# Expert matmuls of the first layer in tiles of 32 columns, and the first modulation summed in PSUM

## The chip, the cores and the metric

The kernel runs on one core of a Trainium2 chip. The core has five engines that run side by side: TensorE for matmuls (its weight loads are shown apart), VectorE, ScalarE, GpSimd, and SyncE, whose queue issues most of the loads. Sixteen DMA engines move data between HBM and SBUF. Matmuls write to PSUM, which this kernel uses in banks of 128 partitions x 512 float32. The metric is the device time of one execution in microseconds.

## The reference

The reference is one mixing block followed by a two-layer block. All of it is float32, with D = 1024, 512 tokens (the latent ones) and 256 context tokens.

```python
# first block: modulation from the vector c, then norm, affine, projection
mod = silu(c) @ w_ada + b_ada                    # 1024 x 3072
shift, scale, gate = split(mod, 3)
h = rms_norm(x, norm_pre) * (1 + scale) + shift
proj = h @ w_in                                  # then a recurrence and an attention, w_out
...
# in each of two layers, behind its attention: 16 experts, each takes its top tokens
xs = h[idx]                                      # 64 latent tokens, 32 context tokens
a, u = xs @ w_gate[e], xs @ w_up[e]              # 1024 x 1024 each
y = (silu(a) * u) @ w_down[e]                    # 1024 x 1024
out = zeros.at[idx].add(y * gates)
```

In the first layer both latent and context tokens go through the experts (context with its own choice and the same weights); in the second layer only the latent ones do.

## The kernel before

The whole program is one launch. Code is written as generators that are woven together, and a planner puts every engine's instructions into a fixed order, so an engine's order follows the program's where nothing is blocked.

**Start of the first block** (`first`, lines 629 to 704). x is loaded in four tiles, then the first group of w_in (`group_`: load into a ring of two tiles `w`, copy on ScalarE into `hi`, subtraction on GpSimd into `lo`, because each projection is three matmuls on split operands, lines 323 to 325). Then the first modulation runs: `ada` (line 336) takes w_ada in tiles of 128 x 1024 (`wa`, 512 KB; two per k, sixteen for shift and scale) through a ring of four, and for each of eight k makes one matmul per half row (line 364) into column tiles of 32 of a PSUM bank. Here the bank comes from `held`, a pool of one; each k's result is added to `rows` on VectorE (line 366), which gives the bank back. At the end `done1` transposes the rows (line 378) into columns, and A and shift follow. Between the modulation's fourth step and its end stand the small tables: softplus, block weights `wbd`, position and rope tables, mask, then the norm of x and its transposes into `xT`. With A known, xT is scaled (line 698), copied to `h_hi` and subtracted to `h_lo` (lines 699 and 700; odd k on VectorE, even k on GpSimd), and the projection starts.

**Experts** (`experts`, line 1427). Per expert, X is gathered by an indirect DMA (line 1439), transposed (line 1445), and goes as the stationary operand XT (1024 rows in eight k; 64 latent and 32 context columns). Weights come in loads of 1 MB, two k each, through 19 slots (`slot`, line 1406): four pairs for gate and up, then four for down. A slot is loaded again when its matmuls are done. For each k the latent part makes four matmuls into two column tiles of 64 (line 1468) and the context part four into column tiles of 32 (line 1459), in turn; for the last two k the context part comes after both. Then silu on ScalarE, product on VectorE, transposes (lines 1481 and 1493), and the down matmuls: latent in tiles of 64 (line 1503), context in tiles of 32 (line 1518). Results are scaled and added to HBM by indirect DMAs on GpSimd's queue. Four PSUM banks rotate for gate, up, context and the context transposes.

## Time and profile before

| | |
|---|---|
| three runs | 2518.55, 2521.3, 2523.43 us (median 2521.3) |
| profiled execution | 2520.2 us |
| its span, first to last instruction | 2518.4 us |
| TensorE busy | 2134.2 us (85%) |
| TensorE weight loads | 1209.4 us (48%) |
| VectorE, ScalarE, GpSimd busy | 43%, 28%, 23% |
| moved by DMA | 563.86 MB, mean 224 GB/s |

Busy time is an average over stages. The first block and the attentions lie before 950 us and between 1520 and 1950 us, the first layer's experts between 957 and 1525 us, the second layer's between 2009 and 2510 us. A float32 matmul stands in the trace as two records, each with a weight load of its own. Names of engines in rows: PE is TensorE, PEld its weight loads, DVE VectorE, ACT ScalarE, POOL GpSimd, SPq the queue of loads.

### The profile page before, as it was taken

How to read it: one execution, taken by the hardware profiler on the slowest of the kernel's cores; microseconds unless marked ns; L12 is line 12 of the kernel's file. 1: busy time of each engine (PE TensorE's matmuls, PEld its weight loads, DVE VectorE, ACT ScalarE, POOL GpSimd, SP SyncE). 2: the span in 40 equal slices, each digit the busy share in tenths (PEclk: the TensorE clock that was granted, in tenths of full speed). 3: DMA queues.
4: the chain of work that ended last, by engine and by line, in shares of the span. 5: the costliest groups of instructions: out<-in, count | busy, mean ns of one | idle time of the engine just before them, and what ended most of it. 6: DMA issues, size and time to landing. Idle time of an engine off the chain costs nothing. (4 is left out here: it accounts for less than half of the span.)

```text
span 2518.4 us, 32647 instructions
## 1 busy us (share of the span) xinstructions
PE 2134.2 (85%) x12298; PEld 1209.4 (48%) x12298; DVE 1074.1 (43%) x2785; ACT 711.5 (28%) x1642; POOL 586.6 (23%) x804
## 2 busy tenths in 40 slices
PE   5999887999997868999999996599988597767677
PEld 1778666677785752222222224467677332212222
DVE  5476777646869461111111116788784500000000
ACT  3355543445546110000000004455664100000000
POOL 3343232331434311101111003433243200000000
PEclk9999897999998978999999998799999699998889
DMA  8441231422431558999999953033125699999997
GB/s 284 151 135 43 80 122 30 143 79 77 138 103 55 200 209 316 379 386 381 376 376 383 387 209 96 22 103 100 56 77 176 254 385 391 395 394 390 393 404 279
DMA packets 160761, 563.86 MB, mean 224 GB/s; under 512 B 16454, under 2 KB 16710, under 8 KB 160476
## 3 DMA queue, kind: packets, MB, share of 16 engines
q1 hardware_dynamic: 146172, 522.90, 55.8%
q0 software_dynamic: 14432, 38.88, 5.7%
q8 instruction: 97, 1.59, 0.3%
q14 instruction: 60, 0.49, 0.1%
HBM read 538.59 MB, written 23.14 MB: 223 GB/s over the span
## 5 line engine op out<-in xcount | busy, mean ns | idle before, releaser
L1468 PE MATMUL bank<-we,XT 128*64 128x512 f32 x2048 | 507.3, 629 | 94.7 <-DMA we<-in_w_exp_gate_dram 66.0
L1468 PEld LDWEIGHTS bank<-we,XT 128*64 128x64 f32 x2048 | 141.2, 142 | 442.1 <-issue 322.8
L1478 DVE TENSOR_TENSOR sg<-sg,bank 128x512 f32<-128x512 f32 x32 | 22.0, 687 | 646.5 <-PE bank L1468 646.5
L1503 PE MATMUL pbank<-we,hT 128*64 128x512 f32 x1024 | 229.1, 596 | 10.7 <-ACT hT L1483 9.0
L1477 ACT ACTIVATE sg<-bank 128x512 f32<-128x512 f32 x32 | 19.1, 597 | 661.0 <-PE bank L1468 661.0
L1439 POOL DMA_INDIRECT X<-H,gx x32 | 29.9, 934 | 617.6 <-PE bank L1445 553.7
L526 PE MATMUL bank<-cons,p 128*128 128x128 f32 x800 | 127.5, 282 | 27.2 <-ACT pT L252 10.2
L512 DVE TENSOR_REDUCE mx<-bank 128x1 f32<-128x768 f32 (+1 forms) x160 | 134.9, 846 | 35.8 <-PE bank L504 34.5
L515 ACT ACTIVATE p<-bank,mx 128x768 f32<-128x768 f32 (+1 forms) x160 | 130.7, 818 | 58.7 <-DVE mx L512 22.0
L1503 PEld LDWEIGHTS pbank<-we,hT 128*64 128x64 f32 x1024 | 71.5, 137 | 145.6 <-issue 126.2
L1459 PE MATMUL bank<-we,XT 128*32 128x512 f32 x1024 | 133.9, 607 | 0.0
L526 PEld LDWEIGHTS bank<-cons,p 128*128 128x128 f32 x800 | 92.4, 143 | 61.0 <-ACT pT L252 17.6
L268 POOL TENSOR_TENSOR lo<-w,hi 128x1024 fp32r<-128x1024 f32 (+1 forms) x44 | 95.2, 2170 | 98.1 <-ACT hi L267 66.2
L323 PE MATMUL pbank<-hi,h 128*128 128x384 f32 x288 | 101.7, 354 | 7.0 <-ACT vt L1094 3.6
L252 ACT ACTIVATE pT<-bank 128x256 f32<-128x256 f32 (+3 forms) x187 | 84.5, 476 | 70.2 <-PE bank L526 63.7
L325 PE MATMUL pbank<-hi,h 128*128 128x384 f32 x288 | 100.6, 349 | 0.0
L324 PE MATMUL pbank<-lo,h 128*128 128x384 f32 x288 | 100.3, 348 | 0.0
L1507 DVE SCALAR_TENSOR_TENSOR yl<-pbank,gt,m 128x512 f32<-128x512 f32 x32 | 23.9, 748 | 177.9 <-PE pbank L1503 151.5
L504 PE MATMUL bank<-ks,qs 128*128 128x256 f32 (+1 forms) x320 | 83.4, 375 | 12.5 <-ACT p L515 9.1
L268 POOL TENSOR_TENSOR wo_lo<-wo_raw,wo_hi 128x512 fp32r<-128x512 f32 (+1 forms) x40 | 60.7, 1527 | 99.6 <-ACT wo_hi L267 97.5
L504 PEld LDWEIGHTS bank<-ks,qs 128*128 128x128 f32 x320 | 57.1, 205 | 35.3 <-ACT p L515 14.5
L1483 ACT ACTIVATE hT<-pbank 128x512 f32<-128x512 f32 x32 | 19.1, 597 | 183.5 <-PE pbank L1481 183.5
(444 smaller groups left out, 4204.6 us busy)
## 6 DMA issues: line engine op xcount, KB each, us to landing
we<-in_w_exp_down_dram SPq DMA_DIRECT2D x127, 1024.0 KB
we<-in_w_exp_up_dram SPq DMA_DIRECT2D x124, 1024.0 KB
we<-in_w_exp_gate_dram SPq DMA_DIRECT2D x123, 1024.0 KB
wa<-in_w_ada_dram SPq DMA_DIRECT2D x120, 512.0 KB
w<-in_w_in_dram SPq DMA_DIRECT2D x24, 512.0 KB
w<-in_w_in_even_dram SPq DMA_DIRECT2D x20, 384.0 KB
H<-h SPq DMA_DIRECT2D x10, 512.0 KB
we<-in_w_exp_gate_dram POOLq DMA_DIRECT2D x5, 1024.0 KB, 10.9
```

Source lines behind the costliest of these rows:

```text
L252: self.nc.scalar.activation(out, ps, AF.Copy)
L268: (engine or self.nc.gpsimd).tensor_sub(lo, w, hi)
L323: t.matmul(ps, lhsT=lhs[0], rhs=rhs[0], start=start, stop=False)
L324: t.matmul(ps, lhsT=lhs[0], rhs=rhs[1], start=False, stop=False)
L325: t.matmul(ps, lhsT=lhs[1], rhs=rhs[0], start=False, stop=stop)
L504: self.nc.tensor.matmul(ps[:, a - k0:b - k0], lhsT=qs[:, q0:q0 + 128], rhs=ks[:, a:b], start=i == 0, stop=i == len(passes) - 1)
L512: nc.vector.tensor_reduce(m, ps, axis=AX, op=OP.max, negate=True)
L515: nc.scalar.activation(p, ps, AF.Exp, bias=m, accum_out=den)
L526: self.nc.tensor.transpose(ps[:, a - b:a - b + 128], p[:, a:a + 128], self.ident)
L1459: nc.tensor.matmul(pc[q:q + 32], lhsT=XT[:, k, 64:96], rhs=w[:, k % 2, 512 * h:512 * h + 512], start=k == 0, stop=k == 7)
L1468: nc.tensor.matmul(ps[64 * h:64 * h + 64], lhsT=XT[:, k, :64], rhs=w[:, k - k0, 512 * h:512 * h + 512], start=k == 0, stop=k == 7)
L1503: nc.tensor.matmul(py[64 * h:64 * h + 64], lhsT=hT[:, j, 64 * kh:64 * kh + 64], rhs=w[:, 512 * h:512 * h + 512], start=j == 0 and kh == 0, ...
```

## The change

In the first layer's experts, gate and up go into three banks. Each bank holds, for one group of 32 tokens (two groups latent, one context), up and gate in four column tiles of 32; in the second bank gate and up change places. All four column tiles are written in turn, and so are those of the down matmuls, for latent as for context. Silu and product run once for each bank. The second layer's experts keep their tiles of 64. In both layers the up weights of a pair are loaded before the gate weights, and the functions are split up.

In the first block the modulation's weights are loaded right behind x, through a ring of nine tiles, ahead of the first group of w_in, the tables and the block weights. Where a `held` bank is given, the sum over k stays in PSUM and is added to `rows` once. x is transposed into the tile Y, which is otherwise first written later.

```diff
@@ -333,12 +333,12 @@
                 yield


-    def ada(self, w, b, stat, nmod, nvec, pool, ring, banks, done, bank=None, bufs=None):
+    def ada(self, w, b, stat, nmod, nvec, pool, ring, banks, done, held=None, bufs=None):
+


         nc = self.nc
         wv = w.rearrange("(k p) n -> p k n", p=128)
-        bank = bank or self.pbank
         wt = [None, None]

         def load(bk, k):
@@ -359,11 +359,16 @@
             load(bk, 0)
             yield
             for k in range(8):
-                ps = bank()
+                if not held:
+                    ps = self.pbank()
+                elif k == 0:
+                    ps = held()
                 for t in range(2 * len(mods)):
                     nc.tensor.matmul(ps[32 * t:32 * t + 32, :], lhsT=stat[:, k, :],
-                                     rhs=wt[t // 2][:, (t % 2) * 512:(t % 2 + 1) * 512], start=True, stop=True)
-                nc.vector.tensor_add(rows[:n], ps[:n], rows[:n])
+                                     rhs=wt[t // 2][:, (t % 2) * 512:(t % 2 + 1) * 512],
+                                     start=not held or k == 0, stop=not held or k == 7)
+                if not held or k == 7:
+                    nc.vector.tensor_add(rows[:n], ps[:n], rows[:n])
                 if k < 7:
                     load(bk, k + 1)
                 yield
@@ -660,15 +665,32 @@
         mask = mk.tile([128, 512], F32, name="mask")
         k2 = self.pool("f_k2")
         xp = self.pool("f_x")
-        sring = self.pool("f_sring", 4)
+        sring = self.pool("f_sring", 9)
         xt = xp.tile([128, 4, D], F32, name="x")
         for t in range(4):
             nc.sync.dma_start(out=xt[:, t], in_=I["x"][t * 128:(t + 1) * 128, :])
         stat = self.stationary(self.col("c"), 1, "stat1", ap)
         ada1 = lambda banks, ring: self.ada(I["w_ada"], I["b_ada"], stat, 3, 1, ap, ring, banks, done1, held)
+        mods = ada1((0,), sring)
+        drain(take(mods, 5))
+        xT = Y[:, :, :S]
+        for t in range(4):
+            r = self.tile_rstd(xt[:, t], xp.tile([128, D], BF16, name="junk", bufs=1))
+            v.tensor_scalar(xt[:, t], xt[:, t], r, None, op0=OP.mult)
+        drain(take(mods, 2))
+        for k in range(8):
+            ps = self.bank()
+            for t in range(4):
+                nc.tensor.transpose(ps[:, t * 128:(t + 1) * 128], xt[:, t, k * 128:(k + 1) * 128], self.ident)
+            self.evac(xT[:, k], ps)
+        drain(mods)
         w = drain(self.group_(I["w_in_0"]))
-        mods = ada1((0,), sring)
-        drain(take(mods, 4))
+        for k in range(8):
+            v.tensor_scalar(xT[:, k], xT[:, k], A[:, k:k + 1], mod[:, 0, 0, k:k + 1], op0=OP.mult, op1=OP.add)
+            nc.scalar.activation(hi[:, k], xT[:, k], AF.Copy)
+            (v if k % 2 else nc.gpsimd).tensor_sub(lo[:, k], xT[:, k], hi[:, k])
+        sring.release()
+        xp.release()
         sp = self.softplus_neg(self.col("lam"), k2)
         spc = k2.tile([128, 2, 4], F32, name="spc")
         v.tensor_scalar(spc[:, 0], sp, 2.0, None, op0=OP.mult)
@@ -684,23 +706,6 @@
                 nc.sync.dma_start(out=wbd[64 * b:64 * b + 64, j, :, 64 * b:64 * b + 64], in_=wg[b])
         cs, sn = self.first_rope_tables(k2)
         nc.sync.dma_start(out=mask, in_=I["mask"])
-        xT = xp.tile([128, 8, S], F32, name="xT")
-        for t in range(4):
-            r = self.tile_rstd(xt[:, t], xp.tile([128, D], BF16, name="junk", bufs=1))
-            v.tensor_scalar(xt[:, t], xt[:, t], r, None, op0=OP.mult)
-        for k in range(8):
-            ps = self.bank()
-            for t in range(4):
-                nc.tensor.transpose(ps[:, t * 128:(t + 1) * 128], xt[:, t, k * 128:(k + 1) * 128], self.ident)
-            self.evac(xT[:, k], ps)
-        drain(mods)
-        for k in range(8):
-            v.tensor_scalar(xT[:, k], xT[:, k], A[:, k:k + 1], mod[:, 0, 0, k:k + 1], op0=OP.mult, op1=OP.add)
-            nc.scalar.activation(hi[:, k], xT[:, k], AF.Copy)
-            (v if k % 2 else nc.gpsimd).tensor_sub(lo[:, k], xT[:, k], hi[:, k])
-        sring.release()
-        xp.release()
-
         scr = self.pool("f_scr")
         sc = self.pool("f_sc", side="right")
         stk = self.pool("f_stk", 2, side="right")
@@ -1449,97 +1453,129 @@
...
-            pg, pu = self.bank(), self.bank()
-            pc = self.bank() if ctx else None
-
-            def gate_up_ctx(k, wg, wu):
-                for j, w in enumerate((wu, wg)):
-                    for h in range(2):
-                        q = 64 * j + 32 * h
-                        nc.tensor.matmul(pc[q:q + 32], lhsT=XT[:, k, 64:96],
-                                         rhs=w[:, k % 2, 512 * h:512 * h + 512], start=k == 0, stop=k == 7)
-
-            for k0 in range(0, 8, 2):
-                wg = load(I["w_exp_gate_2"][i, e], k0)
-                wu = load(I["w_exp_up_2"][i, e], k0)
-                for k in range(k0, k0 + 2):
-                    for ps, w in ((pg, wg), (pu, wu)):
-                        for h in range(2):
-                            nc.tensor.matmul(ps[64 * h:64 * h + 64], lhsT=XT[:, k, :64],
-                                             rhs=w[:, k - k0, 512 * h:512 * h + 512], start=k == 0, stop=k == 7)
-                    if ctx and k < 6:
-                        gate_up_ctx(k, wg, wu)
-            if ctx:
-                for k in (6, 7):
-                    gate_up_ctx(k, wg, wu)
...
+            last = e + 1 == EXPERTS
+            XT = (self.expert_ctx if ctx else self.expert_lat)(i, e, R, wk, XT, None if last else prep)
...
+    def expert_weights(self, i, e, k0):
+        I = self.I
+        return self.load_expert(I["w_exp_up_2"][i, e], k0), self.load_expert(I["w_exp_gate_2"][i, e], k0)
+
...
+    def expert_ctx(self, i, e, R, wk, XT, prep):
+
+
+        nc, v = self.nc, self.nc.vector
+        bg = [self.bank() for _ in range(3)]
+        for k0 in range(0, 8, 2):
+            wu, wg = self.expert_weights(i, e, k0)
+            for k in range(k0, k0 + 2):
+                for g in range(3):
+                    for q in range(4):
+                        w = ((wu, wg), (wg, wu))[g == 1][q // 2]
+                        nc.tensor.matmul(bg[g][32 * q:32 * q + 32], lhsT=XT[:, k, 32 * g:32 * g + 32],
+                                         rhs=w[:, k - k0, 512 * (q % 2):512 * (q % 2) + 512],
+                                         start=k == 0, stop=k == 7)
+        wd = self.expert_down(i, e)
+        sg = wk.tile([128, 512], F32, name="sg")
+        sc = wk.tile([64, 512], F32, name="sc")
+        nc.scalar.activation(sg[:64], bg[0][64:], AF.Silu)
+        v.tensor_mul(sg[:64], sg[:64], bg[0][:64])
+        nc.scalar.activation(sg[64:], bg[1][:64], AF.Silu)
+        v.tensor_mul(sg[64:], sg[64:], bg[1][64:])
+        nc.scalar.activation(sc, bg[2][64:], AF.Silu)
+        v.tensor_mul(sc, sc, bg[2][:64])
+        XTn = prep and prep(e + 1)
+        ps = self.pbank().rearrange("p (a c) -> p a c", a=4)
+        for j in range(4):
+            nc.tensor.transpose(ps[:, j], sg[:, j * 128:(j + 1) * 128], self.ident)
+        hT = wk.tile([128, 4, 128], F32, name="hT")
+        nc.scalar.activation(hT, ps, AF.Copy)
+        ps = self.bank().rearrange("p (a c) -> p a c", a=4)
+        for j in range(4):
+            nc.tensor.transpose(ps[:, j, :64], sc[:, j * 128:(j + 1) * 128], self.ident[:64, :64])
+        hc = wk.tile([128, 4, 64], F32, name="hc")
+        nc.scalar.activation(hc, ps[:, :, :64], AF.Copy)
+
+        def latent():
+            py = self.pbank()
+            for kh in range(2):
+                for j in range(4):
+                    w = wd[2 * kh + j // 2][:, j % 2]
+                    for d in range(2):
+                        for g in range(2):
+                            q = 64 * d + 32 * g
+                            c = 64 * g + 32 * kh
+                            nc.tensor.matmul(py[q:q + 32], lhsT=hT[:, j, c:c + 32], rhs=w[:, 512 * d:512 * d + 512],
+                                             start=j == 0 and kh == 0, stop=j == 3 and kh == 1)
+            yl = wk.tile([128, 512], F32, name="yl")
+            v.scalar_tensor_tensor(yl, py, R["gt"][:, e:e + 1], R["m5"], op0=OP.mult, op1=OP.mult)
+            self.scatter(R, e, yl, 0)
+
+        def context():
...
+        for f in (latent, context) if prep else (context, latent):
+            f()
+        return XTn
```

Not shown: `expert_lat`, `expert_down` and `scatter`, which hold the old latent code, and `context`, which is the old `down_ctx`. In `ada2` the argument `bank` is renamed to `held`.

## Rows read from the trace of the kernel before

**Rows 1.** The page: its span.
```profile
span 2518.4 us, 32647 instructions
```

**Rows 2.** Windows: length; busy of PE, PEld, DVE, ACT, POOL; PEclk, DMA share, GB/s.
```profile
1030.01:1065.28 35.27, 34.98 (x212) 9.88 (x209) 4.41 (x6) 2.77 (x5) 3.95 (x3) 1.00 1.01 380
...
2100.00:2150.00 50.00, 39.96 (x186) 13.06 (x184) 3.51 (x5) 1.79 (x3) 2.19 (x3) 0.93 1.03 402
```

**Rows 3.** Waits of the load queue, 955 to 1480 us: total, times, longest.
```profile
SPq L1416 <- PE bank L1459: 318.5, 60, 40.8
```

**Rows 4.** Time line of PE, 48 to 70 us: start, duration, instruction, count, wait.
```profile
50.76 1.53 PE L364 MATMUL held<-wa,stat 128*32 128x512 f32 x4 [1.51 <-DMA wa<-in_w_ada_dram]
...
56.11 0.69 PE L323 MATMUL pbank<-hi,h_hi 128*128 128x384 f32 x1
...
69.05 0.34 PE L323 MATMUL pbank<-hi,h_hi 128*128 128x384 f32 x1
```

**Rows 5.** Time line of PE, one expert of the first layer.
```profile
1030.01 1.94 PE L1468 MATMUL bank<-we,XT 128*64 128x512 f32 x8
1031.88 1.06 PE L1459 MATMUL bank<-we,XT 128*32 128x512 f32 x8
...
1047.19 3.65 PE L1468 MATMUL bank<-we,XT 128*64 128x512 f32 x16
1050.78 1.92 PE L1459 MATMUL bank<-we,XT 128*32 128x512 f32 x16
1052.63 0.88 PE L1445 MATMUL bank<-cons,X 96*128 96x96 f32 x8
...
1054.69 7.09 PE L1503 MATMUL pbank<-we,hT 128*64 128x512 f32 x32
1061.71 3.64 PE L1518 MATMUL pbank<-we,hc 128*32 128x512 f32 x32
1065.28 1.94 PE L1468 MATMUL bank<-we,XT 128*64 128x512 f32 x8
```

**Rows 6.** Time line, last expert of the first layer, behind its gate and up.
```profile
1511.30 0.59 ACT L1486 ACTIVATE sc<-bank 64x512 f32<-64x512 f32 x1 [2.14 <-PE bank L1459]
...
1511.92 0.68 DVE L1487 TENSOR_TENSOR sc<-sc,bank 64x512 f32<-64x512 f32 x1 [1.74 <-ACT sc L1486]
...
1512.66 0.46 PE L1493 MATMUL bank<-cons,sc 64*128 64x64 f32 x4 [0.84 <-DVE sc L1487]
```

**Rows 7.** Expert loads, first layer's end and all; last expert's first down matmul.
```profile
L1416 SPq DMA_DIRECT2D we<-in_w_exp_down_dram x9: 368/387/1309, 1400.5 to 1471.0; - x9
...
DMA to landing us min/median/max: 5.7/11.2/20.5
...
1513.65 3.64 PE L1518 MATMUL pbank<-we,hc 128*32 128x512 f32 x32 [0.53 <-ACT hc L1495]
```

**Rows 8.** Time line of the load queue, first 25 us.
```profile
10.09 4.17 SPq L348 DMA_DIRECT2D wa<-in_w_ada_dram  x4
```

**Rows 9.** Windows of the start (columns of rows 2).
```profile
0.00:6.50 6.50, 0.00 (x0) 0.00 (x0) 0.96 (x10) 3.72 (x6) 2.12 (x8) 1.00 0.58 167
6.50:18.00 11.50, 3.73 (x10) 1.22 (x10) 11.02 (x61) 7.57 (x12) 4.20 (x2) 1.00 1.03 410
18.00:52.00 34.00, 21.59 (x86) 5.54 (x86) 13.45 (x39) 8.18 (x13) 10.17 (x5) 0.94 0.93 323
```

**Rows 10.** Groups by line to 64 us (count, busy, mean ns, idle); one stalled product.
```profile
L268 POOL TENSOR_TENSOR lo<-w,hi 128x1024 fp32r<-128x1024 f32 x6 | 14.4, 2406 | 30.2 <-ACT hi L267 30.2
...
L700 POOL TENSOR_TENSOR h_lo<-xT,h_hi 128x512 fp32r<-128x512 f32 x4 | 5.4, 1380 | 2.4 <-ACT h_hi L699 2.4
...
16.55 2.27 DVE L242 TENSOR_TENSOR rs_t<-rs_t,rs_h 128x1 f32<-128x1 f32 x1
```

**Rows 11.** Windows of dense instructions; the count stands behind each engine's busy time.
```profile
1796.00:1836.00 40.00, 38.98 (x327) 31.39 (x326) 31.24 (x88) 23.73 (x65) 15.52 (x42) 1.00 0.11 35
...
1823.80:1833.80 10.00, 10.00 (x94) 9.16 (x95) 9.38 (x32) 7.15 (x25) 6.24 (x15) 1.00 0.01 2
```

More of the change, by code (lines that the diff above doesn't have):

```diff
@@ L413, in done, with steps @@
                                                op0=OP.add, op1=OP.mult)
-        def steps(banks, stat, pool, ring, bank=None):
-            return self.ada(I["w_ada_2"][i], I["b_ada_2"][i], stat, 6, 2, pool, ring, banks, done, bank, 2)
+        def steps(banks, stat, pool, ring, held=None):
+            return self.ada(I["w_ada_2"][i], I["b_ada_2"][i], stat, 6, 2, pool, ring, banks, done, held, 2)
         return (A, mod[:, :, 0, :]), rowd, steps
@@ L1434, in experts @@
         wk = self.pool(f"moe{i}", 2)
-        load = self.load_expert
         def prep(e):
@@ L1497, in down_lat @@
-            def down_lat():
-                py = self.pbank()
-                for kh in range(2):
-                    for j in range(4):
-                        w = wd[2 * kh + j // 2][:, j % 2]
-                        for h in range(2):
-                            nc.tensor.matmul(py[64 * h:64 * h + 64], lhsT=hT[:, j, 64 * kh:64 * kh + 64],
-                                             rhs=w[:, 512 * h:512 * h + 512],
-                                             start=j == 0 and kh == 0, stop=j == 3 and kh == 1)
-                yl = wk.tile([128, 512], F32, name="yl")
-                v.scalar_tensor_tensor(yl, py, R["gt"][:, e:e + 1], R["m5"], op0=OP.mult, op1=OP.mult)
-                nc.gpsimd.indirect_dma_start(out=R["acc"][0], in_=yl, in_offset=None, compute_op=OP.add,
-                                             out_offset=bass.IndirectOffsetOnAxis(ap=R["sx"][:, e:e + 1], axis=0))
@@ L1542, in experts, with expert_down, scatter @@
             return t
+    def expert_weights(self, i, e, k0):
+        I = self.I
+        return self.load_expert(I["w_exp_up_2"][i, e], k0), self.load_expert(I["w_exp_gate_2"][i, e], k0)
+    def expert_down(self, i, e):
+        return [self.load_expert(self.I["w_exp_down_2"][i, e], k0) for k0 in range(0, 8, 2)]
+    def scatter(self, R, e, y, part):
+        acc, idx = R["acc"][part], R[("sx", "cx")[part]]
+        self.nc.gpsimd.indirect_dma_start(out=acc, in_=y, in_offset=None, compute_op=OP.add,
+                                          out_offset=bass.IndirectOffsetOnAxis(ap=idx[:, e:e + 1], axis=0))
```

91 lines of the change are left out of this document (45 added, 46 removed).

## Prediction

> **What bounds the kernel now.** I read the page first, then the time windows of the two expert stages, the time line of one expert, the waits of the load queue, and last the time line of the first 70 us. The page gives a span of 2518.4 us, in which TensorE is busy 85% [rows 1]. The profiled execution took 2520.2 us, 1.8 us more than its span; the median of the three runs shown is 2521.3 us, 1.1 us above it. About 0.2% (5 us) is what a measurement of this kernel can tell from no change.
>
> The share is an average over stages, and the edits touch two of them. In the first layer's expert stage TensorE is busy 34.98 of 35.27 us, at the full 2.4 GHz, while the DMA engines also show a share of 1.01 and 380 GB/s [rows 2]: both look full. The queue tells them apart. Of some 525 us, the load queue spends 318.5 us waiting for the gate/up matmuls alone to give a slot back [rows 3], so TensorE sets the pace and the loads follow it. In the second layer's experts it is the other way round: TensorE is busy 39.96 of 50 us, and DMA is at 1.03 and 402 GB/s [rows 2]. That stage's matmuls do not change, only the order of its first two loads.
>
> At the start the first modulation waits for its weights: the last of their matmuls begin at 50.76 us, the first projection starts at 56.11 us, and its 24th matmul, as many as one pass over the eight k has, starts at 69.05 us [rows 4]. All later work hangs on that pass.
>
> **The expert edit.** One expert is one period of the time line, 1030.01 to 1065.28 us [rows 5]. Two runs of each kind give the cost of a record and of a change of kind (a float32 matmul is two records). Tiles of 64: eight records take 1.87 us, sixteen 3.59 us (1047.19 to 1050.78), so a record costs 0.215 us, and 0.15 us more are paid once a block. Tiles of 32: sixteen records take 1.85 us and 32 take 3.57 us, so 0.1075 us each and 0.13 us a block. A record of 64 costs exactly two of 32; splitting it is free, and what goes is the cost per block, 0.14 us.
>
> Gate and up now take 22.61 us (1030.01 to 1052.63): 64 records x 0.215 + 64 x 0.1075 = 20.64 us, and 1.98 us for 14 blocks. After the change, 192 records x 0.1075 = 20.64 us and one block, 20.78: 1.84 us less. The down matmuls take 10.59 us (1054.69 to 1065.28): 32 x 0.215 + 32 x 0.1075 = 10.32 and two block costs. After it, 96 x 0.1075 = 10.32, and nothing is paid between latent, context and the next gate/up: 0.27 us less. Between them lie 2.06 us of transposes and waits, in which the new order of silu and product must not lose. Sum: 35.27 - 1.84 - 0.27 = 33.16 us, 2.11 us less, times 16 experts = 34 us.
>
> The middle piece: silu and product run three times where they ran twice, one more silu (0.59 us) and product (0.68 us). In the last expert the context chain ends it today: its silu starts at 1511.30, its product ends at 1512.60, and the transposes start at 1512.66 [rows 6]. The new first bank is complete two groups (8 records each, 1.72 us) before the third, the second one group (0.86 us) before it, so the two earlier silus end before the third starts, and the second product ends some 0.6 us after the last matmul, under the 0.88 us of the next expert's transposes [rows 5]. I cost it at nothing; both ends: a gain is excluded because the third chain is the old one, and without that cover it is 0.59 + 0.68 = 1.27 us an expert, 20 us. The Trainium skill (TensorEngine Tiling (Array Packing), section PSUM Bottleneck) warns that after tiling the copies out of PSUM may become the bound; by it the sum would lose up to those 20 us, by the rows nothing.
>
> Will the loads keep up? Per expert DMA moves 13.4 MB (380 GB/s x 35.27 us), and 33.16 us would ask for 404 GB/s, about what the second layer's window shows with less scatter. Take the worst, that 35.27 us is already DMA's floor. Then it falls 2.11 us behind per expert, 34 us in all. But it is ahead: the last expert's weights are issued by 1471.0 us and its first down matmul starts at 1513.65 us, 42 us later; less the longest landing shown, 20.5 us (few loads have a landing time), 22 us of lead are left, and 31 us with the median 11.2 us [rows 7]. So the loss is between 0 and 34 - 22 = 12 us. I take 0, as the second layer shows DMA above 380 GB/s.
>
> The wu load goes before wg, though wg's matmuls come first in the second layer: up to four records (0.86 us) are done later per pair of loads. They lie under DMA's pace there; at nothing to 1 us once, nothing.
>
> **The start.** Today the queue issues x, two loads of w_in_0 and the bias rows before its first four of w_ada at 10.09 us [rows 8]; block weights in small pieces, position, mask and more of w_in go between the other twelve. DMA runs at 410 GB/s between 6.5 and 18 us and at 323 GB/s after that [rows 9]. After the change, only the small tables, x and 16 loads of w_ada are ahead of the last one: 0.6 + 2.1 + 8.4 = 11.1 MB. 1.1 MB are through at 6.5 us (167 GB/s); 10 MB at 410 GB/s need 24 us: landed at about 31 us, at 323 GB/s at 37 us. I take 32. From the last matmuls (50.76) to the first projection (56.11) are 5.35 us today, so the projection could begin at 37.4.
>
> What is late next is w_in_0, now behind w_ada. Its four loads pass a ring of two; each costs a copy on ScalarE and a subtraction of 2.41 us on GpSimd, which also has four of 1.38 us for h [rows 10]. From about 34 us (landing and copy of the first) that is 4 x 2.41 + 4 x 1.38 = 15.2 us on GpSimd, and some 2 us for the ring's turn: the first pass ends at about 52 instead of 69 us, 17 us earlier. Against it: VectorE slows beside GpSimd (a 128x1 product took 2.27 us at 16.55 us, otherwise 0.16 [rows 10]), and the block weights, mask and tables of the rope now come later, beside h. Bounds: 18 us if only w_ada's landing counts (50.76 - 32), nothing if the splits and tables fill the time. I take 14, near the GpSimd row. Later stages wait for other engines, not for a date, so they move along.
>
> The held sum removes 7 of 8 adds per bank. Where such an add held TensorE up, that stall is in the start already; the rest lies beside an idle VectorE (13.45 of 34 us busy [rows 9]). Nothing. x transposed into Y costs nothing: Y is first written much later.
>
> **Sum.** 2520.2 - 34 - 14 = 2472 us for the profiled execution, 2473 for the median.
>
> **Rivals.** (a) The start gains little: w_in_0, its splits and the small loads arrive as late as the modulation did. For it: GpSimd's 15 us in a row; against: the 19 us by which w_ada lands earlier. 2521 - 34 - 3 = 2484.
> (b) The silu chain or the loads take back part of the expert gain: 12 to 20 us, 2485 to 2493. Against it: the two earlier banks and the 22 us of lead.
> (c) Slower: TensorE's issue becomes the bound in the experts. An expert has 212 records today and 308 after, each with a weight load of its own: 576 instructions in 31.1 us, 54 ns each, with DMA full. Above (35.27 - 2.06) / 576 = 57.6 ns an expert gets slower, and with the start's 14 us the kernel above 59 ns. For it: one of the densest long stretches, 40 us from 1796.00, has 327 + 326 = 653 instructions, 61.3 ns each, busy or not. Against it: 94 + 95 = 189 in 10 us, 53 ns each [rows 11]. At 61.3 ns an expert takes 35.3 + 2.06 = 37.4 us, 34 us more in all, less 14: 2541. The Trainium skill (TensorE: Matmul & The Clock Gate, section Wait — 56ns, not 53.3ns?) gives about 62 ns per MATMUL for a sequencer that decodes in microcode; were that paid for every instruction, weight loads included, the time would be 2547 us. The stretch with 53 ns speaks against that reading.
> (d) No change: planned order or loads eat both gains, 2521.
>
> **Chances.** As forecast 0.62 (2460 to 2482), (a) 0.14, (b) 0.10, (c) 0.08, (d) 0.06. Faster 0.86, same 0.06, slower 0.08. The range 2460 to 2494 takes in the forecast, (a) and (b), and leaves out (c) and (d).
>
> **What would show it.** Right: an expert period near 33.2 us, one unbroken stretch of 192 gate/up records at 0.1075 us, no DMA wait in front of them, the first pass over k complete near 52 us. Wrong: gate/up records above 0.115 us each, idle time before the transposes of the latent half, TensorE waiting for expert weights in the last experts, or the first projection waiting for w_in_0 past 60 us.

## The result, and the profile after

The changed kernel takes 2480.2 us (median of 4 runs, 2479.8 to 2484.7) against 2522.2 us for the kernel before beside it: ratio 0.9844, 95% interval 0.983 to 0.9858, which is 39 us less, 36 to 43; the two medians are 42 us apart. The prediction was 2473 us, range 2460 to 2494. The profiled execution took 2480.4 us with a span of 2478.6 us.

The first layer's experts first. Time line of TensorE over one expert of the changed kernel (start, duration, instruction, count, wait), against [rows 5]:

```profile
1050.47 20.78 PE L1522 MATMUL bank<-we,XT 128*32 128x512 f32 x192
1071.19 0.88 PE L1449 MATMUL bank<-cons,X 96*128 96x96 f32 x8
1071.90 0.60 PE L1537 MATMUL pbank<-cons,sg 128*128 128x128 f32 x4
1072.71 0.46 PE L1542 MATMUL bank<-cons,sc 64*128 64x64 f32 x4 [0.21 <-DVE sc L1533]
1073.25 7.07 PE L1555 MATMUL pbank<-we,hT 128*32 128x512 f32 x64
1080.14 3.62 PE L1568 MATMUL pbank<-we,hc 128*32 128x512 f32 x32
1083.58 6.62 PE L1522 MATMUL bank<-we,XT 128*32 128x512 f32 x60
```

Gate and up are one stretch of 192 records in 20.78 us, nothing waits in front of it, and the period is 33.11 us where it was 35.27. The prep is the transposes of the next expert's X (L1449, 0.88 us). The only wait inside is 0.21 us in front of the context's transposes: the third product ends just behind the prep, as it did before.

Windows of one expert in the first layer and of 50 us in the second (length; busy of PE, PEld, DVE, ACT, POOL; PEclk, DMA share, GB/s), against [rows 2]:

```profile
1050.47:1083.58 33.11, 32.82 (x309) 10.66 (x305) 5.09 (x7) 3.35 (x6) 3.96 (x3) 1.00 1.03 389
2060.00:2110.00 50.00, 43.11 (x192) 14.03 (x192) 3.51 (x5) 2.03 (x4) 3.38 (x3) 0.93 1.03 403
```

Waits of the load queue during the first layer's experts (total, times, longest), against [rows 3]:

```profile
SPq L1421 <- PE bank L1522: 170.0, 55, 37.5
```

TensorE still sets the pace there, but the margin has shrunk: the loads wait 170 us for its gate/up matmuls instead of 318.5.

The last expert of that layer has no following prep to hide its products. Its time line, all engines, against [rows 6]:

```profile
1468.32 0.69 DVE L1531 TENSOR_TENSOR sg<-sg,bank 64x512 f32<-64x512 f32 x1 [0.17 <-ACT sg L1530]
...
1469.06 0.66 PE L1537 MATMUL pbank<-cons,sg 128*128 128x128 f32 x4 [0.58 <-DVE sg L1531]
...
1469.91 0.46 PE L1542 MATMUL bank<-cons,sc 64*128 64x64 f32 x4 [0.20 <-DVE sc L1533]
```

Here TensorE does stand 0.58 us for the second bank's product, once in the kernel; in the other fifteen the 0.88 us of prep covers it.

Now the start. Time line of TensorE, against [rows 4]:

```profile
39.05 3.90 PE L367 MATMUL held<-wa,stat 128*32 128x512 f32 x12 [1.50 <-DMA wa<-in_w_ada_dram]
...
48.41 0.44 PE L323 MATMUL pbank<-hi,h_hi 128*128 128x384 f32 x1 [2.90 <-ACT h_hi L690]
...
56.47 0.69 PE L325 MATMUL pbank<-hi,h_lo 128*128 128x384 f32 x1 [2.91 <-DVE h_lo L691]
...
60.64 0.33 PE L323 MATMUL pbank<-hi,h_hi 128*128 128x384 f32 x1
```

The first projection begins 7.7 us earlier (48.41 for 56.11) and its 24th matmul 8.4 us earlier (60.64 for 69.05), not 17. The start of that 24th record is what this text calls the first pass. It is a mark of progress and not the end of a whole pass: nine of the 24 are of the first kind (L323), and the records on VectorE's last difference, which ends at 63.7 us, begin at 63.76 us, without a wait of TensorE. Two views say why the gain is small. Time line of the load queue, against [rows 8]:

```profile
7.73 6.54 SPq L348 DMA_DIRECT2D wa<-in_w_ada_dram  x9
14.31 1.43 SPq L286 DMA_DIRECT2D w<-in_w_in_dram  x2
17.72 1.82 SPq L706 DMA_DIRECT2D wbd<-in_w_rg_a_dram  x2
...
21.53 1.61 SPq L348 DMA_DIRECT2D wa<-in_w_ada_dram  x2
...
27.63 0.33 SPq L708 DMA_DIRECT2D mask<-in_mask_dram  x1
28.26 4.77 SPq L348 DMA_DIRECT2D wa<-in_w_ada_dram  x7
33.12 1.17 SPq L286 DMA_DIRECT2D w<-in_w_in_dram  x2
```

Windows of the start, columns as above, against [rows 9]:

```profile
18.00:24.00 6.00, 6.00 (x34) 2.41 (x33) 1.29 (x2) 1.95 (x4) 0.00 (x0) 1.00 1.03 412
24.00:30.00 6.00, 2.59 (x20) 1.01 (x16) 0.00 (x0) 3.31 (x5) 2.69 (x2) 0.88 1.08 276
30.00:37.00 7.00, 5.57 (x16) 0.71 (x16) 3.58 (x14) 0.91 (x3) 1.95 (x1) 0.61 1.03 393
```

The sixteen loads of w_ada are not together. With the ring of nine full in its plan, the planner put two loads of w_in_0, the block weights in pieces of 256 bytes and the mask behind the ninth. Between 24 and 30 us the DMA engines are full (1.08) and move 276 GB/s.

Time lines of VectorE, then GpSimd, behind the modulation, against [rows 10]:

```profile
45.16 10.65 DVE L689 TENSOR_SCALAR Y<-Y,A,mod 128x512 f32<-128x512 f32 x8
55.74 7.94 DVE L691 TENSOR_TENSOR h_lo<-Y,h_hi 128x512 fp32r<-128x512 f32 x4
```

```profile
45.07 4.85 POOL L268 TENSOR_TENSOR lo<-w,hi 128x1024 fp32r<-128x1024 f32 x2
49.88 1.45 POOL L691 TENSOR_TENSOR h_lo<-Y,h_hi 128x512 fp32r<-128x512 f32 x1
52.36 2.71 POOL L691 TENSOR_TENSOR h_lo<-Y,h_hi 128x512 fp32r<-128x512 f32 x2 [1.02 <-ACT h_hi L690]
```

In the kernel before, the same eight products read

```profile
54.85 6.63 DVE L698 TENSOR_SCALAR xT<-xT,A,mod 128x512 f32<-128x512 f32 x8
```

VectorE is busy without a gap from 45.16 to 63.7 us; the prediction had no term for it. Its eight products take 1.33 us each where they took 0.83, while GpSimd works beside them for 8.9 of the 10.65 us.

Adding up by stage: the first expert begins 7.9 us earlier (946.4 for 954.3), the first layer's experts last 536.1 us where they lasted 571.1 (from the first prep to the last scatter), 35.0 less; between the layers nothing changes (483.8 and 484.0 us); and the second layer's experts last 3.3 us longer, 506.1 for 502.8. Together 39.6 of the span's 39.8 us.

### The profile page after: what moved, and what is told of

Read it like the earlier page. It is cut to its first block, busy times and chain, and to the rows that moved or that the text cites. A ratio compares the mean times of both kernels' runs of the same rounds, so it can differ in the third digit from the quotient of the medians.

```text
span 2478.6 us, 35664 instructions
## 1 busy us (share of the span) xinstructions
PE 2085.6 (84%) x13834; PEld 1214.1 (49%) x13834; DVE 1076.7 (43%) x2780; ACT 721.5 (29%) x1658; POOL 587.9 (24%) x804
## 4 chain that ended last, share of the span: by engine, by line
PE 57%; DMA 16%; DVE 14%; ACT 5%; issue 5%; POOL 2%; SPq 1%; POOLq 0%; DVEq 0%; ACTq 0%
PE bank L1522 13%; DMA we<-in_w_exp_gate_dram 6%; PE pbank L323 5%; PE pbank L325 5%; PE pbank L324 5%; PE bank L1486 4%; PE pbank L1555 4%; PE bank L509 4%; DMA we<-in_w_exp_up_dram 3%; PE bank L539 3%; PE pbank L1503 2%; PE pbank L1568 2%; PE bank L531 2%; DMA we<-in_w_exp_down_dram 2%; PE pbank L367 2%
## 5 line engine op out<-in xcount | busy, mean ns | idle before, releaser
L1522 PE MATMUL bank<-we,XT 128*32 128x512 f32 x3072 | 334.8, 595 | 1.1 <-DVE XT L1451 1.1
L1486 PE MATMUL bank<-we,XT 128*64 128x512 f32 x1024 | 252.3, 629 | 92.1 <-DMA we<-in_w_exp_gate_dram 77.8
L1522 PEld LDWEIGHTS bank<-we,XT 128*32 128x32 f32 x3072 | 99.7, 111 | 232.8 <-issue 229.1
L1486 PEld LDWEIGHTS bank<-we,XT 128*64 128x64 f32 x1024 | 76.1, 144 | 255.7 <-issue 149.2
L1451 DVE COPY XT<-bank 128x768 f32<-128x768 f32 (+1 forms) x32 | 26.1, 817 | 280.3 <-PE bank L1486 148.5
L1503 PE MATMUL pbank<-we,hT 128*64 128x512 f32 x512 | 122.2, 618 | 14.3 <-ACT hT L1496 9.0
L1529 DVE TENSOR_TENSOR sg<-sg,bank 64x512 f32<-64x512 f32 x16 | 10.9, 679 | 283.1 <-ACT sg L1528 283.1
L1490 ACT ACTIVATE sg<-bank 128x512 f32<-128x512 f32 x16 | 9.6, 597 | 360.0 <-PE bank L1486 360.0
L1555 PE MATMUL pbank<-we,hT 128*32 128x512 f32 x1024 | 113.2, 594 | 1.1
L323 PE MATMUL pbank<-hi,h 128*128 128x384 f32 x288 | 100.0, 348 | 6.4 <-DVE mix L959 3.1
L1528 ACT ACTIVATE sg<-bank 64x512 f32<-64x512 f32 x16 | 9.5, 594 | 320.7 <-PE bank L1522 320.7
```

Of the source, the lines that this page charges most:

```text
L323: t.matmul(ps, lhsT=lhs[0], rhs=rhs[0], start=start, stop=False)
L1486: nc.tensor.matmul(ps[64 * h:64 * h + 64], lhsT=XT[:, k], rhs=w[:, k - k0, 512 * h:512 * h + 512], start=k == 0, stop=k == 7)
L1503: nc.tensor.matmul(py[64 * h:64 * h + 64], lhsT=hT[:, j, 64 * kh:64 * kh + 64], rhs=w[:, 512 * h:512 * h + 512], start=j == 0 and kh == 0, ...
L1522: nc.tensor.matmul(bg[g][32 * q:32 * q + 32], lhsT=XT[:, k, 32 * g:32 * g + 32], rhs=w[:, k - k0, 512 * (q % 2):512 * (q % 2) + 512], star ...
L1555: nc.tensor.matmul(py[q:q + 32], lhsT=hT[:, j, c:c + 32], rhs=w[:, 512 * d:512 * d + 512], start=j == 0 and kh == 0, stop=j == 3 and kh == 1)
```

## The experiments

All times are medians beside runs of the kernel before on the same chip; the changed kernel stands at ratio 0.9844.

**The experts alone.** The start of the kernel before, the experts of the changed one.

```diff
-            pg, pu = self.bank(), self.bank()
...
+            XT = (self.expert_ctx if ctx else self.expert_lat)(i, e, R, wk, XT, None if last else prep)
```

> The expert edit alone; the start is that of the kernel before (block weights and w_in_0 early, ring of four, an add for each k). Theory (the cost per change of tile kind goes, TensorE's issue is no bound, and the second layer's experts give some 3 us back because up is now loaded ahead of gate): period of the first layer's experts 33.1 us, that layer 35 us shorter, the second layer's experts 506 us as in the changed kernel: 2522 - 35 + 3 = 2490 us, ratio 0.987. Rival (the 3 us come from the changed start or from chance, not from the order of loads): second layer's experts 503 us, 2487 us, ratio 0.986. Rival (part of the 35 us is the start's): period above 33.5 us, over 2493 us.

Measured: 2485.6 us against 2518.3, ratio 0.9863 (0.9848 to 0.9877). TensorE's time line shows the expert of the changed kernel:

```profile
1090.56 20.78 PE L1517 MATMUL bank<-we,XT 128*32 128x512 f32 x192
...
1113.34 7.07 PE L1550 MATMUL pbank<-we,hT 128*32 128x512 f32 x64
```

Period 33.1 us, first layer 535.1 us (36.0 less), second layer's experts 504.8 us (2.0 more). The expert edit is worth 33 us by the medians and 34 by the ratio (31 to 38), and the stage shows it under the start of the kernel before. The time cannot tell 0.986 from 0.987, and 504.8 us lies between the 503 and 506 expected, so the 3 us are left to the gate-first run below.

**The start alone.** The start of the changed kernel, the experts of the one before.

```diff
-        sring = self.pool("f_sring", 4)
+        sring = self.pool("f_sring", 9)
...
+                                     start=not held or k == 0, stop=not held or k == 7)
```

> The start alone (held sum, ring of nine, w_in_0 and block weights behind x and the first five steps), the experts as before. Theory: first pass over k complete near 60.6 us as in the changed kernel, experts' period 35.27 us, second layer's experts 503 us since gate is loaded first there: 2522 - 8 = 2514 us, ratio 0.997. Rival (the 3 us lost in the second layer belong to the start's edit): 506 us there, 2517 us, ratio 0.998.

Measured: 2510.9 us against 2518.3, ratio 0.9971 (0.996 to 0.9983): 7.3 us, 4 to 10. First pass at 61.5 us, second layer's experts 502.5 us. So the start's edit gains about half of the predicted 14 us, and the loss in the second layer does not come with it. The two ratios multiply to 0.983, the changed kernel's within the intervals.

**Blocks of one tile kind.** The kernel before with its tiles of 64 and 32, in 8 blocks in place of 14.

```diff
-                    if ctx and k < 6:
-                        gate_up_ctx(k, wg, wu)
-            if ctx:
-                for k in (6, 7):
-                    gate_up_ctx(k, wg, wu)
+                if ctx:
+                    for k in range(k0, k0 + 2):
+                        gate_up_ctx(k, wg, wu)
```

> The kernel before with its tiles of 64 and 32 kept, but the context's matmuls of two k put together behind the latent's of the same two: 8 blocks of one tile kind in place of 14 in gate and up. Theory (the cost is paid per change of tile kind, 0.14 us each): period 35.27 - 6 x 0.14 = 34.43 us, 16 x 0.84 = 13 us less, ratio 0.995. Rival (what gained in the changed kernel is the tile of 32 as such, or the order of the banks): 35.27 us, ratio 1.000.

Measured: 2504.0 us against 2518.4, ratio 0.9938 (0.9917 to 0.996). TensorE's time line, one expert's last blocks and the next one's first:

```profile
1031.17 1.92 PE L1459 MATMUL bank<-we,XT 128*32 128x512 f32 x16
...
1047.48 1.92 PE L1459 MATMUL bank<-we,XT 128*32 128x512 f32 x16
1049.34 0.88 PE L1445 MATMUL bank<-cons,X 96*128 96x96 f32 x8
...
1061.99 3.65 PE L1468 MATMUL bank<-we,XT 128*64 128x512 f32 x16
1065.57 1.92 PE L1459 MATMUL bank<-we,XT 128*32 128x512 f32 x16
```

Period 34.41 us from prep to prep (34.40 from 1031.17 to 1065.57): 0.86 us less for six changes of kind, 0.143 us each, without a single matmul of another shape. That is the price the prediction read off [rows 5], now measured by itself. At this price the fifteen changes that the changed kernel saves in an expert come to 2.15 us, and its period is 2.16 us shorter; nothing is left for the tile of 32 as such. The Trainium skill (TensorEngine Tiling (Array Packing), section Key Properties) says that changing the tiling mode drains TensorE; the trace shows a fixed price at each change, which agrees, but no view shows the drain itself.

**Half the columns per matmul**, to see how far off TensorE's issue is.

```diff
-                        nc.tensor.matmul(bg[g][32 * q:32 * q + 32], lhsT=XT[:, k, 32 * g:32 * g + 32],
...
+                        for f in range(0, 512, 256):
+                            nc.tensor.matmul(bg[g][32 * q:32 * q + 32, f:f + 256], lhsT=XT[:, k, 32 * g:32 * g + 32],
...
+                                             start=k == 0 and f == 0, stop=k == 7 and f == 256)
```

> The changed kernel with each gate/up matmul of the first layer cut in two of 256 columns: 384 records where there were 192, each with a weight load, for the same columns. Theory (columns bound it, and TensorE takes instructions much faster than they come now): period 33.1 us as before the cut, 2480 us. Rival (an instruction costs 54 ns or more, weight loads among them): 768 x 0.054 = 41.5 us for gate and up in place of 20.8, period 54 us, 330 us more. Between them (only a matmul has a floor, of 60 ns say): 384 x 0.06 = 23 us, period 35.4 us, 37 us more.

Measured in one run: 2489.4 us beside 2518.7 for the kernel before. TensorE's time line:

```profile
990.45 20.97 PE L1523 MATMUL bank<-we,XT 128*32 128x256 f32 x384
...
1023.68 8.67 PE L1523 MATMUL bank<-we,XT 128*32 128x256 f32 x156
```

384 records and as many weight loads in 20.97 us: 27 ns an instruction, and 0.0546 us for a record of half the columns. The period is 33.23 us. Its first layer's experts last 539.2 us, 3.1 more; the rest of the 9 us between this one run and the changed kernel's median lies mostly ahead of them, for the first expert begins at 952.2 us. Twice the instructions in gate and up cost 0.2 us an expert, so the changed kernel's 54 ns an instruction are far from a bound of issue, and rival (c) is refuted and not only unseen. The Trainium skill (TensorE: Matmul & The Clock Gate, section Wait — 56ns, not 53.3ns?) gives about 62 ns per MATMUL for decoding in microcode; 54.6 ns from one matmul to the next, with a weight load between, is less, so that case is not the one here.

**Gate ahead of up again**, otherwise the changed kernel.

```diff
-        return self.load_expert(I["w_exp_up_2"][i, e], k0), self.load_expert(I["w_exp_gate_2"][i, e], k0)
+        wg = self.load_expert(I["w_exp_gate_2"][i, e], k0)
+        return self.load_expert(I["w_exp_up_2"][i, e], k0), wg
```

> The changed kernel with gate loaded ahead of up again, in both layers. Theory: the second layer's experts, where the gate matmuls come first and DMA sets the pace, fall from 506 to 503 us: 2477 us, 3 less than the changed kernel, ratio 0.983. The first layer keeps its period of 33.1 us, as its loads are well ahead. Rival (the order of two loads costs nothing under DMA's pace): 506 us there and 2480 us, ratio 0.9844.

Measured: 2477.3 us against 2518.3, ratio 0.9834 (0.982 to 0.9848), which the times cannot tell from 0.9844. The stage can. In this kernel TensorE's first prep and GpSimd's last scatter of the second layer stand at

```profile
1971.13 1.11 PE L1449 MATMUL bank<-cons,X 64*128 64x64 f32 x8 [4.88 <-DMA X<-H,gx]
```

```profile
2475.03 1.55 POOL L1475 DMA_INDIRECT out_dram<-yl,sx  x1 [11.67 <-DVE yl L1508]
```

and in the changed kernel at

```profile
1966.28 1.11 PE L1449 MATMUL bank<-cons,X 64*128 64x64 f32 x8 [4.75 <-DMA X<-H,gx]
```

```profile
2472.39 1.55 POOL L1474 DMA_INDIRECT out_dram<-yl,sx  x1 [10.26 <-DVE yl L1507]
```

That is 503.9 and 506.1 us. Over all profiles of this study, five kernels with gate first last 502.5 to 503.9 us there (mean 503.0), nine with up first 504.8 to 508.1 (mean 506.1), whatever their start: the order of two loads costs 3 us. From this kernel to the changed one, TensorE's waits for gate grow from 69 to 78 us and those for up shrink from 26 to 14, so the sum of the two does not explain it. Nor is the pace of the loads lost. The queue issues that stage's last load, in this kernel and then in the changed one, at

```profile
2442.67 0.42 SPq L1421 DMA_DIRECT2D we<-in_w_exp_down_dram  x1
```

```profile
2437.18 0.42 SPq L1421 DMA_DIRECT2D we<-in_w_exp_down_dram  x1
```

That is 471.5 and 470.9 us behind the first prep, and the same holds for all (470.3 to 471.5 us with gate first, 469.5 to 470.9 with up first). The 3 us show behind it: the last gate/up matmul begins 491.4 to 492.9 us behind the first prep with gate first and 493.3 to 494.9 with up first, the last down matmul 500.8 to 502.2 and 503.2 to 506.4. The two groups also differ in the order of gate, up and down among the last ten loads; what in it costs the 3 us stays open.

**Block weights late.** They get a pool in the place of x and w_ada's ring, so their loads fall behind all of w_ada.

```diff
         xp.release()
+        kw = self.pool("f_kw")
...
...
-        wbd = k2.tile([128, 2, 4, 128], F32, name="wbd")
+        wbd = kw.tile([128, 2, 4, 128], F32, name="wbd")
...
```

> The changed kernel with the block weights in a pool that takes the place of x and of w_ada's ring, so that their loads in pieces of 256 bytes go behind all sixteen of w_ada. Theory: in the changed kernel these pieces let DMA fall from 412 to 276 GB/s between 24 and 30 us, which is 6 x 136 / 412 = 2.0 us, with their own bytes 2.6 us; the last w_ada and w_in_0 land that much earlier, the first pass over k is complete near 58 us instead of 60.6, 2478 us, ratio 0.9834. Rival (VectorE's and GpSimd's chain of products and splits sets the first pass): complete at 60 to 61 us, 2480 us. Rival (the block weights now come late, behind the products): the second pair of w_in_0, queued behind them, is late, over 62 us, and 2482 us or more.

Measured: 2474.0 us against 2518.3, ratio 0.9819 (0.9804 to 0.9834). Its window of the start, and TensorE's time line:

```profile
24.00:30.00 6.00, 3.20 (x22) 1.16 (x20) 3.90 (x6) 4.26 (x5) 3.98 (x3) 1.00 1.03 403
```

```profile
43.46 0.45 PE L323 MATMUL pbank<-hi,h_hi 128*128 128x384 f32 x1 [0.91 <-ACT h_hi L690]
...
53.67 0.69 PE L325 MATMUL pbank<-hi,h_lo 128*128 128x384 f32 x1 [4.01 <-DVE h_lo L691]
...
60.00 0.33 PE L323 MATMUL pbank<-hi,h_hi 128*128 128x384 f32 x1
```

The pieces do cost the landing what was expected: 403 instead of 276 GB/s, VectorE's add that ends the modulation stands 3.0 us earlier (40.09 for 43.05 us), and the first projection begins 4.95 us earlier. But the first pass is at 60.0 us, 0.6 us earlier, which is within the spread of equal programs (below): TensorE now waits 4.01 us for VectorE's h_lo. The rival is right about the first pass. The time is 6 us lower than the changed kernel's, which this does not explain.

**w_in_0 ahead of w_ada.**

```diff
+        w = drain(self.group_(I["w_in_0"]))
         stat = self.stationary(self.col("c"), 1, "stat1", ap)
...
-        w = drain(self.group_(I["w_in_0"]))
```

> The changed kernel with w_in_0 loaded ahead of w_ada again; held sum, ring of nine and the later block weights stay. Theory (what counts for the first pass is the sum of the bytes of x, w_ada and w_in_0, and VectorE's chain behind them): w_ada lands some 2 us later, but w_in_0's splits are done by then, and VectorE's eight products take 0.83 us each instead of 1.33, 4 us less; first pass over k complete between 58 and 61 us, 2478 to 2480 us. Rival (w_ada's landing decides, as the prediction had it): first pass 4 to 5 us later than 60.6, 2484 us, ratio 0.986.

Measured: 2482.6 us against 2518.4, ratio 0.9861 (0.984 to 0.9882), first pass at 65.4 us, the rival's number. Its reason holds in part: the modulation ends 2.6 us later (VectorE's add at 45.65 us), and the first pass 4.8 us. The theory failed: with w_in_0's splits done, GpSimd took the next group's (4.84 us from 47.66), and VectorE's products took 10.65 us as in the changed kernel.

**Four of the eight products on ScalarE.**

```diff
+            if k % 2:
+                nc.scalar.activation(xT[:, k], xT[:, k], AF.Identity, scale=A[:, k:k + 1], bias=mod[:, 0, 0, k:k + 1])
+            else:
...
```

> The changed kernel with four of the eight products that make h put on ScalarE, the others left on VectorE. Theory (VectorE sets the first pass: from 45.16 us it runs eight products of 1.33 us and four differences of 2 us beside GpSimd's splits): VectorE has 5.3 us less to do, GpSimd's own chain ends at 56 us, so the first pass is complete at 56 to 57 us instead of 60.6, 2476 to 2477 us, ratio 0.983. Rival (GpSimd's splits and the landing of w_in_0 set it): 60 to 61 us, 2480 us.

Measured: 2479.4 us against 2518.4, ratio 0.9837 (0.9817 to 0.9856); first pass at 58.3 us, between the theory's 56 to 57 and the rival's 60 to 61. VectorE's time line:

```profile
44.56 7.87 DVE L692 TENSOR_SCALAR Y<-Y,A,mod 128x512 f32<-128x512 f32 x4
```

Half the products, yet 7.87 us of VectorE for them, 1.97 us each: what is long is not the work, it is the time for which GpSimd goes on, which here works throughout.

**No GpSimd in this stretch.** The differences for h and w_in_0's splits all on VectorE, which so has more to do.

```diff
-            self.split(hi, lo, w)
+            self.split(hi, lo, w, self.split_on)
...
+        self.split_on = v
         w = drain(self.group_(I["w_in_0"]))
+        self.split_on = None
...
-            (v if k % 2 else nc.gpsimd).tensor_sub(lo[:, k], xT[:, k], hi[:, k])
+            v.tensor_sub(lo[:, k], xT[:, k], hi[:, k])
```

> The changed kernel with the differences for h and the splits of w_in_0 all on VectorE, none on GpSimd. Theory (VectorE's products stand still while GpSimd works: in the changed kernel eight take 10.65 us, 8.9 of them with GpSimd busy, and with four of the products moved to ScalarE the other four still took 7.87 us): products 0.3 us each, 2.4 us, eight differences at 0.63 us, 5 us, two splits of 1.3 us; VectorE is through at about 55 us instead of 63.7 though it does more, first pass over k complete at 56 to 57 us instead of 60.6, 2476 us, ratio 0.983. Rival (VectorE's share of the work was the bound, and more work makes it later): over 62 us, 2482 us or more.

Measured: 2467.8 us against 2518.7, ratio 0.9804 (0.979 to 0.9817). VectorE's time line:

```profile
44.08 1.22 DVE L269 TENSOR_TENSOR lo<-w,hi 128x1024 fp32r<-128x1024 f32 x1
...
46.43 3.73 DVE L692 TENSOR_SCALAR Y<-Y,A,mod 128x512 f32<-128x512 f32 x8
50.08 4.89 DVE L694 TENSOR_TENSOR h_lo<-Y,h_hi 128x512 fp32r<-128x512 f32 x8
```

The same eight products take 3.73 us in place of 10.65, eight differences 4.89 us where four took 7.94, and VectorE is through at 55.0 us instead of 63.7 with more work. The first pass, however, is only at 59.4 us, 1.3 us earlier, not 4: next in line is TensorE, whose queue has a matmul of the second modulation in front, waiting 1.74 us for its weights at 51.07 us, and then eleven records at 0.32 us from one to the next, with a granted clock of 0.50 (1.2 GHz) from 53.4 to 56.9 us, after stretches in which TensorE stood idle; later ones, at a granted clock of 1.00 from 58 us, take 0.17. The changed kernel has such records too (0.32 us apart from 56.95 to 59.2 us). So only a small part of what this kernel gains over the changed one (0.9844 to 0.9804, 10 us) is the first pass; more on the rest below.

**An add for each k again**, in the changed kernel.

```diff
-                if not held:
-                    ps = self.pbank()
-                elif k == 0:
-                    ps = held()
+                ps = (held or self.pbank)()
...
-                                     start=not held or k == 0, stop=not held or k == 7)
-                if not held or k == 7:
-                    nc.vector.tensor_add(rows[:n], ps[:n], rows[:n])
+                                     start=True, stop=True)
+                nc.vector.tensor_add(rows[:n], ps[:n], rows[:n])
```

> The changed kernel with the modulations' partial sums added on VectorE for every k again, in the held bank's pool, the order of loads and the ring of nine left as they are. Theory (the held sum in itself is worth nothing; an add of 0.69 us goes beside the wait for the next load): 2480 us, ratio 0.984. Rival (the adds held TensorE up between loads): up to 7 x 0.69 = 5 us more at the start, 2485 us, ratio 0.986.

Measured: 2473.0 us against 2518.7, ratio 0.9822 (0.9808 to 0.9835); first pass at 64.8 us, 4.2 us later. TensorE's time line shows waits on the adds:

```profile
39.24 1.93 PE L364 MATMUL held<-wa,stat 128*32 128x512 f32 x8 [0.80 <-DVE ada_rows L367]
...
58.44 1.92 PE L364 MATMUL held<-wa,stat 128*32 128x512 f32 x4 [6.99 <-DVE ada_rows L367]
```

The second line is the dear one: an add of the second modulation stands behind the products on VectorE, and the first projection stands behind that modulation's next matmul on TensorE. At the start the held sum is worth 3 to 4 us (64.8 us against 60.5 to 61.5 in four equal programs, below), near the rival's number, though the longest wait is not the one between loads that the rival named; the whole kernel is yet not slower.

**A ring of four.**

```diff
-        sring = self.pool("f_sring", 9)
+        sring = self.pool("f_sring", 4)
```

> The changed kernel with w_ada's ring at four again instead of nine; everything else stays. Theory (the ring is what lets the plan put w_ada's loads together): the plan now puts the block weights after the fourth load and three to four loads of w_in_0 and of the next group among the other twelve, so the last load of w_ada lands 3 to 5 us later, the first projection begins at 51 to 53 us instead of 48.4, the first pass over k is complete at 63 to 65 us, and most of the start's gain is gone, 2482 to 2484 us, ratio 0.986. Rival (the queue keeps a limited number of loads in flight anyway, so slots bind nothing): w_ada lands as in the changed kernel, first pass near 60.6 us, 2480 us, ratio 0.984.

Measured: 2478.0 us against 2517.5, ratio 0.9839 (0.9826 to 0.9852). VectorE's eight products read

```profile
53.79 6.66 DVE L689 TENSOR_SCALAR Y<-Y,A,mod 128x512 f32<-128x512 f32 x8
```

First projection at 55.1 us, first pass at 65.9, both later than the theory had them, so the ring is what brings w_ada forward; but 5.3 us at the first pass are not seen in the time, which is the rival's.

**Three together**: block weights late, no GpSimd in the stretch, gate ahead of up; the edits are those above.

> The changed kernel with three things together: block weights loaded late, the differences of h and of w_in_0 all on VectorE, and gate loaded ahead of up. Theory (the block weights hold up the landing by 3 us, GpSimd holds up VectorE's products by 4 us or more, up ahead of gate costs the second layer 3 us): first projection at 43 to 44 us, first pass complete at 52 to 53 us, second layer's experts 503 us, 2469 to 2471 us, ratio 0.980. Rival (each of these is hidden behind the next wait): 2474 us or more, ratio over 0.982.

Measured: 2461.4 us against 2518.7, ratio 0.9776 (0.9763 to 0.979), 57 us less than the kernel before, the best of the study. First projection 43.8 us as expected, first pass 55.6 where 52 to 53 was, second layer's experts 502.7 us. The time is 8 us below the lower end expected; 5 us of that are the stretch described next.

**Where first pass and time part.** Take the stretch from the last projection ahead of the first layer's attention (TensorE, `pbank<-hi,h`, at 752.1 us in the changed kernel) to the first expert. In three kernels (no GpSimd, three together, an add for each k) it lasts 188.7 to 189.0 us. TensorE's instructions stand in one and the same order there in these three, and in another one, all but the same for all, in the other eleven profiles, where it lasts 190.2 to 196.1 us (mean 194.2; 194.1 in the kernel before, 194.3 in the changed one). None of the three edits touches that stretch; the order planned for it is another one. So some 5 us of their gain is not what they were made to test. That is half of why the add for each k looks no slower: its first expert begins 6.3 us earlier than the changed kernel's, though its first pass comes 4.1 us later.

The rest is of the size by which equal programs differ. Four kernels have one and the same order of TensorE's instructions up to the first expert (changed, start alone, gate first, half the columns): first pass at 60.6, 61.5, 60.5 and 61.3 us, first expert at 946.4, 943.6, 950.9 and 952.2. Three have that of the kernel before (it, experts alone, blocks of one kind): first pass at 69.1, 66.2 and 67.1 us, first expert at 954.3, 954.4 and 954.5. So the changed start is worth 6.4 us at the first pass between the two means, where the profiled pair alone shows 8.4, and between 2 and 11 us at the first expert. A few us at the start cannot be read from the time, and differences under 1 to 3 us cannot be read from one first pass.

## Why the prediction was right, and where its size was off

**The expert edit, 34 us: right in mechanism and size.** Period forecast 33.16 us, measured 33.11, and term by term: gate and up 20.72 us (20.78 forecast), the piece between 2.06 (2.06), the down matmuls 10.33 (10.32); stage 35.0 us shorter. The price per block was confirmed by itself (0.143 us for 0.14), the unbroken stretch is there at 0.108 us a record. That the silus and products cost nothing held for fifteen experts of sixteen, and 0.58 us in the last. That the loads keep up held: 389 GB/s, which is 12.9 MB an expert where 13.4 was reckoned, and TensorE waits for no expert weights there. Rival (b) had a narrow cover against it, the 0.88 us of prep; rival (c) had a wide one, 27 ns against 54.

**The load order, "at nothing": mis-sized.** It costs 3 us in the second layer, three times the upper bound given. That bound was reckoned from four records later per pair of loads, "once", under DMA's pace. That pace is indeed kept up to the last load; the 3 us show behind it, and by what path is not settled.

**The start, 14 us: the term that failed.** It gained 8.4 us at the first pass in the profiled pair (6.4 between the means of equal programs), 7.3 us in the time by itself. Two steps of it were wrong. "Only the small tables, x and 16 loads of w_ada are ahead of the last one": the queue had two loads of w_in_0, the block weights and the mask, 1.6 MB, between them, and the pieces of 256 bytes held DMA at 276 GB/s. So the last twelve records on w_ada began at 39.05 us, where the landing was forecast at 32. And the first pass was reckoned by GpSimd's 15 us in a row, from 34 us; GpSimd's last two splits began at 45 us, since the third and fourth loads of w_in_0 came last, and held up VectorE's products, which had no term at all though the text named a stalled product of 2.27 us in [rows 10]. What counts is that splits stand beside the products: with the ring of four, where they are done by then, the products took 6.66 us; with w_in_0 first, where the next group's splits stand there, 10.65 again.

**The held sum, "nothing": wrong.** It is worth 3 to 4 us at the first pass, because an add on VectorE can stand behind other work of VectorE there; "an idle VectorE" was read from a mean over 34 us.

Chances: the forecast case (2460 to 2482) came true, 2 us inside its upper end, and not by errors that cancel: the two terms that missed, the start and the load order, both missed on the slow side. Rival (a), a start that gains little, was half true. Start and load order together put the time 7 us above the forecast.

## What to carry to other kernels

Order matmuls by tile kind before changing their size: read the price of a change off the time line (two runs of each kind), count the changes, and the gain follows to a few per cent (2.11 us forecast for the period, 2.16 measured). When an edit moves loads, read the queue that the planner then makes, for every slot it thinks full is filled with something else; and when it moves a split or a subtraction to GpSimd's time, look at what VectorE does in those microseconds. A gain of a few microseconds at the start must be read at its stage, and there from several profiles, since a new plan further down and the spread of equal programs are as large.

## What the runs showed of the hardware

Eight products of 128x512 on VectorE take 3.73 us with GpSimd idle, 6.66 us with GpSimd at work for 4.3 of them, and 10.65 us with GpSimd at work for 8.9: 0.68 to 0.78 of GpSimd's time is added, as if VectorE stood still for most of it. The Trainium skill (SBUF — State Buffer, section Who interferes with whom) says that VectorE's two-port modes and GpSimd lock one shared pair of ports for a whole instruction; the added time agrees with that in the main, but no view shows the ports. It can go the other way: in the kernel without GpSimd in this stretch, two splits of a later group on GpSimd took 8.60 us beside VectorE's differences. In the changed kernel, where VectorE's differences took 2 us each, the two splits beside them took 5.56 us.

TensorE took 27 ns an instruction, matmuls and weight loads alternating, over 768 instructions: 20.97 us for columns that take 20.78 us with half the instructions.
